# Work that leaves GpSimd, and a planner that models the SBUF port of VectorE and GpSimd

## The chip, the cores and the metric

The kernel runs on one core of one Trainium2 chip. Each engine of the core (TensorE, VectorE, ScalarE, GpSimd, and SyncE for the DMAs) runs its own list of instructions in order; semaphores join them. The metric is the device time of one execution in microseconds (us), as the median of several runs.

## The reference

The program computes two layers of a generative model over 512 latent tokens of width 1024, with 256 context tokens in front, all in float32. Before each layer and each feed-forward network stands an RMSNorm whose scale and shift come from a conditioning vector; after each, a gated residual.

- Layer 0: four heads of bidirectional gated DeltaNet and four heads of bidirectional gated linear attention, in chunks of 64 tokens, over context and latent tokens.
- Layer 1: a Hyena layer. Two long convolutions over 512 positions, `z = gate * long_conv(z, h_fwd, h_bwd, skip)`, whose filters come from a small sine network of the position; the reference takes them by FFT.
- Each layer's feed-forward network: `(silu(u @ w1) * (u @ w3)) @ w2`, with an inner width of 2816.

## The kernel before, in words

**Split products.** A float32 product is made of three faster ones: each operand is split into a rounded part `hi` (ScalarE copies it with a cast) and a rest `lo = x - hi` (VectorE subtracts), and TensorE adds hi·hi, hi·lo and lo·hi in one PSUM bank (`mm3`). So nearly every operand of TensorE costs one ScalarE and one VectorE instruction.

**Order.** Nothing is issued while the program is written down. `Recorder.add` makes an `Op` of each call, with its engine, its dependences and a cost from a formula by engine, operation and size (`cost`, line 404). `schedule` (line 467) then plays the five engines in time: the engine that can start first takes, of the operations that are ready, the one with the best key, which is the longest path of costs behind it plus an offset from the table `BOOST` by section and engine (`"f1@vector"` is VectorE's part of filter chunk 1). DMAs are ordered so too. It also gives out the eight PSUM banks. `issue` writes the instructions out in the order of their planned starts. On the chip that order is fixed for each engine; the true times follow from semaphores. Since `issue` calls every engine from one place, all instructions carry the same line (648) in the profile, and all tiles are named `t` (SBUF) or `bank` (PSUM).

**Stages**, by the time of the profiled execution; neighbours overlap.

- 0 to 250 us: the condition vectors, the input norm, and the Hyena filters in four chunks of 256 channels (`filter_chunk`, sections `f0` to `f3`) for two orders. `fhalf` multiplies four blocks of filter values by a window on VectorE; `mk` (line 937) makes the sum or difference of two blocks, 128x256, on GpSimd: 8 for each chunk and order, 64 in all, 16 of which then overwrite one row with a 1x256 copy. The result is split, `fq` multiplies it by a table of the discrete Fourier transform, and DMAs put the spectra into DRAM (`kscr`). For each chunk and order GpSimd also copies one spectrum (128x256) and one row of it.
- 0 to 600 us: layer 0. `gdn_merge` puts 12 blocks (32x192) a head in place with GpSimd copies, 48 in all, and joins them with small products on TensorE. `gdn_scan` runs both directions of a head chunk by chunk: product, VectorE, product, ScalarE copy `u`, product, VectorE state. For each of its 40 state updates GpSimd scales a block of keys, 128x128, by a column.
- 600 to 1000 and 1300 to 1640 us: the two feed-forward networks. Slices of `w1` and `w3` go through a seven-product scheme of 2x2 blocks (`unit`, line 1830). Of each slice the weight sums S1, S2 and S4 are made on VectorE and the difference S3 (128x512) on GpSimd, 21 for each layer; each is split before TensorE takes it.
- 1000 to 1300 us: Hyena. `project` makes three projections and mirrors blocks of x1 with 16 GpSimd copies, 128x128; `group` transforms, multiplies by the spectra, transforms back and gates. The last gate `y * x2` (128x512) is on GpSimd, 8 times.

Kept on GpSimd in both kernels: the decays, the masks, squares of keys, the gates of layer 0, the sums of products in `conv`, the first gate of Hyena (128x1024) and all memsets.

Of the kernel before, what the change touches and what calls it, by code (L numbers as in the profile page):

```python
# [32 lines left out]
BOOST = {"": 1200, "@gpsimd": 19800, "@vector": -113900, "c": -161700, "c@gpsimd": 173900, "c@sync": -82400,  # L33
         "dft": 21800, "dft@scalar": 56000, "dft@sync": 21800, "dft@vector": -318200, "end": 12900,
         "end@scalar": -111300, "end@sync": -75800, "end@tensor": 253300, "end@vector": 46500, "f0": -3200,
# [19 lines left out]
         "fb@scalar": 22200, "fb@tensor": -4600, "fb@vector": 7200, "ffn0": -123100, "ffn0@scalar": 54200,  # L55
# [5 lines left out]
         "h3@scalar": 117400, "h@sync": 7500, "h@tensor": -117000, "h@vector": -38300, "ht@scalar": 11900,  # L61
         "ht@tensor": 89700, "hy": -14100, "hy@scalar": 26800, "hy@sync": 111000, "hy@tensor": -100100,
         "hy@vector": -3900, "hyout": -1600, "hyout@scalar": -23500, "hyout@sync": -38900, "hyout@vector": -24700,
# [10 lines left out]
         "m15@tensor": 4100, "m15@vector": 55800, "mlp": 9500, "mlp@scalar": 51700, "mlp@sync": -11600,  # L74
         "mlp@tensor": 29000, "modc": 40000, "modc@tensor": -1400, "modc@vector": -2300, "mods": 148900,
         "mods@sync": 12100, "mods@tensor": 6000, "mods@vector": -1900, "n0": 1900, "n0@gpsimd": -6000,
# [3 lines left out]
         "out@scalar": -2900, "out@sync": 7000, "out@tensor": 177300, "p0": -22500, "p0@gpsimd": -483000,  # L80
# [152 lines left out]


class Op:
    __slots__ = ("eng", "calls", "cost", "deps", "succ", "vts", "prio", "path", "idx", "nd", "bytes", "start", "end", "ready", "sec", "tbl", "anc", "alias", "inst", "rows", "first", "last")


class EngineProxy:
# [445 lines left out]
class Kern:  # L685
# [228 lines left out]
    def filter_chunk(s, c):  # L914
# [22 lines left out]
        def mk(h, t, op, fix=None):  # L937
            x = s.t([P, CW])
            (nc.gpsimd.tensor_add if op > 0 else nc.gpsimd.tensor_sub)(x, h[:, t], h[:, 2 + t])
            if fix is not None:  # L940
                nc.gpsimd.tensor_copy(x[:1], fix)
# [1431 lines left out]
```

## Time and profile before

| What | us |
|---|---|
| three runs | 1673.51, 1678.25, 1680.84 |
| their median | 1678.25 |
| profiled execution | 1673.98 |
| its span, first to last instruction | 1672.3 |

The mean granted TensorE clock was 0.972 in it. Its busy times by engine are the first group of rows below.

Busy time is the time in which an engine holds an instruction; one that waits inside an instruction counts as busy. PE is TensorE, DVE VectorE, ACT ScalarE, POOL GpSimd, SP SyncE. The granted clock is a share of 2.4 GHz: 1.0 or 0.5 at any moment, a mean over a stretch. The DMA queue of SyncE moved 199.39 MB, with the 16 DMA engines busy for 39.5% of the span.

### The profile page before, as it was taken

To read this page: it belongs to the slowest core of one execution; us is meant where nothing else is said; L and a number is where in the kernel's file an instruction comes from. 1 tells how busy PE (TensorE), PEld (TensorE's weight loads), DVE (VectorE), ACT (ScalarE), POOL (GpSimd) and SP (SyncE) were. 2 spreads that over 40 slices of the span, in tenths; PEclk is the share of its full clock that TensorE was granted. 3 is DMA by queue.
4 is the path that set the end of the run, shared out by engine and by line. 5 is a ranking of instruction groups with operands and counts; after the bars stand their busy time and mean duration, and the time that the engine had idled before them with its cause. 6 is when DMAs were issued, how large, how long until landed. Compare 5 with 4: busy or idle time off the path is not lost.

```text
span 1672.3 us, 29141 instructions
## 1 busy us (share of the span) xinstructions
PE 1590.1 (95%) x11356; PEld 1400.8 (84%) x11356; DVE 1248.1 (75%) x2158; ACT 791.1 (47%) x1503; POOL 364.9 (22%) x430
## 2 busy tenths in 40 slices
PE   6999889999999889999999999999999999999998
PEld 3687778778777579989989898888889898989898
DVE  4878985657375886968678688598896977868676
ACT  3556533642434444644536365343344653636353
POOL 0344653513232310101010100143440101011000
PEclk9999997998899889999999999999999999999999
DMA  8744332473266432243343354333432333333331
GB/s 284 208 146 152 108 110 68 160 234 112 75 203 211 130 114 64 82 108 90 88 125 95 109 155 134 97 108 92 133 92 76 102 89 101 99 104 98 106 96 56
DMA packets 257147, 201.25 MB, mean 120 GB/s; under 512 B 11281, under 2 KB 234447, under 8 KB 257008
## 3 DMA queue, kind: packets, MB, share of 16 engines
q1 hardware_dynamic: 257008, 199.39, 39.5%
q8 instruction: 89, 1.46, 0.4%
q14 instruction: 50, 0.41, 0.1%
HBM read 185.70 MB, written 13.66 MB: 119 GB/s over the span
## 4 chain that ended last, share of the span: by engine, by line
PE 64%; DVE 21%; ACT 5%; DMA 4%; issue 3%; POOL 3%; SPq 0%; DVEq 0%; POOLq 0%; ACTq 0%
PE bank L648 64%; DVE t L648 21%; ACT t L648 5%; POOL t L648 3%; DMA t<-in_ffn_w_dram 1%; DMA kscr<-t 0%; SPq L648 0%; DMA t<-in_mod_w_dram 0%; ACT L641 0%; DMA t<-in_dft_filt_dram 0%; DMA t<-in_hy_w_in_dram 0%; DMA t<-in_ctx_dram 0%; DMA t<-gscr 0%; DMA t<-in_hy_w_out_dram 0%; DMA t<-in_dft_fwd_dram 0%
## 5 line engine op out<-in xcount | busy, mean ns | idle before, releaser
L648 PE MATMUL bank<-t 128*128 128x256 f32 (+8 forms) x11356 | 1590.1, 316 | 76.2 <-DVE t L648 47.0
L648 PEld LDWEIGHTS bank<-t 128*128 128x128 f32 (+4 forms) x11356 | 1400.8, 183 | 265.3 <-DVE t L648 72.7
L648 DVE TENSOR_TENSOR t<-t 128x512 fp32r<-128x512 f32 (+11 forms) x1151 | 795.7, 728 | 229.3 <-ACT t L648 150.8
L648 ACT CAST t<-t 128x512 fp32r<-128x512 f32 (+4 forms) x651 | 421.6, 664 | 428.7 <-PE bank L648 203.7
L648 POOL TENSOR_TENSOR t<-t 128x256 f32<-128x256 f32 (+3 forms) x230 | 268.5, 1186 | 952.2 <-DMA t<-in_ffn_w_dram 507.8
L648 ACT ACTIVATE t<-t 128x256 f32<-128x256 f32 (+8 forms) x314 | 156.4, 530 | 151.7 <-DVE t L648 132.0
L648 DVE TENSOR_TENSOR t<-bank,t 128x256 f32<-128x256 f32 (+5 forms) x305 | 147.3, 511 | 63.3 <-PE bank L648 50.7
L648 DVE SCALAR_TENSOR_TENSOR t<-bank,t 128x511 f32<-128x511 f32 (+4 forms) x248 | 143.1, 592 | 52.4 <-PE bank L648 35.4
L648 ACT COPY t<-bank 128x256 f32<-128x256 f32 (+2 forms) x272 | 106.8, 408 | 122.7 <-PE bank L648 119.8
L648 ACT ACTIVATE t<-bank 128x256 f32<-128x256 f32 (+7 forms) x134 | 51.0, 389 | 114.3 <-PE bank L648 111.6
L648 ACT ACTIVATE t<-bank,t 128x512 f32<-128x512 f32 (+3 forms) x94 | 51.2, 557 | 57.5 <-PE bank L648 37.4
L648 POOL COPY t<-t 32x192 f32<-32x192 f32 (+3 forms) x96 | 41.7, 440 | 132.9 <-DVE t L648 112.8
L648 DVE SCALAR_TENSOR_TENSOR t<-t 128x256 f32<-128x256 f32 (+7 forms) x134 | 59.4, 494 | 4.3 <-ACT t L648 3.8
L648 DVE SCALAR_TENSOR_TENSOR t<-t,bank 64x128 f32<-64x128 f32 (+1 forms) x112 | 38.0, 345 | 32.1 <-PE bank L648 29.5
L648 DVE COPY t<-bank 128x256 f32<-128x256 f32 (+8 forms) x70 | 31.2, 456 | 24.9 <-PE bank L648 23.4
L648 POOL TENSOR_SCALAR t<-t 128x128 f32<-128x128 f32 x40 | 31.0, 781 | 64.7 <-PE bank L648 31.5
L641 ACT ACT_TABLE_LOAD x32 | 41.1, 1283 | 1.4 <-PEq L2360 0.8
L648 POOL MEMSET t<- 32x192 f32 (+10 forms) x47 | 18.3, 394 | 78.2 <-PE bank L648 58.9
L648 DVE TENSOR_SCALAR t<-t 128x256 f32<-128x256 f32 (+5 forms) x57 | 23.9, 440 | 3.3 <-ACT t L648 2.8
L648 DVE TENSOR_TENSOR_SCAN t<-t 64x768 f32<-64x768 f32 x8 | 14.0, 1750 | 0.2
L648 DVE STREAM_TRANSPOSE t<-t 128x1024 f32<-128x1024 f32 x6 | 10.4, 1755 | 0.3
L648 POOL TENSOR_SCALAR_AFFINE_SELECT t<-t 128x512 f32<-128x512 f32 (+1 forms) x11 | 6.6, 609 | 13.2 <-DVE t L648 13.2
(15 smaller groups left out, 33.6 us busy)
## 6 DMA issues: line engine op xcount, KB each, us to landing
t<-in_mod_w_dram SPq DMA_DIRECT2D x96, 512.0 KB, 4.0
t<-in_ffn_w_dram SPq DMA_DIRECT2D x88, 512.0 KB, 4.1
t<-in_ffn_w_dram SPq DMA_DIRECT2D x48, 384.0 KB, 3.6
t<-in_ab_w_in_dram SPq DMA_DIRECT2D x28, 512.0 KB
t<-in_hy_w_in_dram SPq DMA_DIRECT2D x24, 512.0 KB, 4.3
kscr<-t SPq DMA_DIRECT2D x72, 128.0 KB, 1.8
t<-kscr SPq DMA_DIRECT2D x24, 256.0 KB, 2.6
t<-in_ffn_w_dram SPq DMA_DIRECT2D x16, 256.0 KB, 2.9
```

Source lines behind the costliest of these rows:

```text
L641: s.nc.scalar.add_instruction(mybir.InstLoadActFuncSet(name=s.nc.get_next_instruction_name(), engine=mybir.EngineType.Activation, act_func ...
L648: r = getattr(getattr(s.nc, o.eng), name)(*[b(x) for x in a], **{n: b(x) for n, x in k.items()})
```

## The change

Five things change.

1. `cost` gives an operation a mark `lock`: on VectorE, where it has more than one SBUF input (columns of scalars not counted), or copies or scales one SBUF tensor without PSUM; on GpSimd, for all but memsets. `schedule` then starts a marked operation no earlier than the planned end of the last marked one on the other engine.
2. The 64 sums of `mk` go from GpSimd to VectorE.
3. The 42 differences S3 and the 8 gates `y * x2` go from GpSimd to VectorE.
4. All copies of `mk`, of the spectrum, of `gdn_merge` and of the mirrored x1 go from GpSimd to ScalarE, and so do the 40 scaled keys of `gdn_scan` (as an activation with a column of scales).
5. The table `BOOST` holds other offsets, for nearly all sections. So the order changes on all engines and in the DMA queue, also far from the moved operations.

```diff
-BOOST = {"": 1200, "@gpsimd": 19800, "@vector": -113900, "c": -161700, "c@gpsimd": 173900, "c@sync": -82400,
...
+BOOST = {"": 65700, "@vector": -50900, "c": -5300, "c@gpsimd": -159000, "c@sync": -2500, "dft": 4600,
...
         elif eng == "vector":
+            sb = sum(1 for x in ins if not isinstance(x, View) and (len(x.shape) > 2 or x.shape[1] > 1))
+            op.lock = op.lock or sb > 1 or (sb == 1 and not ps and name in ("tensor_copy", "tensor_scalar"))
...
         else:
+            op.lock = name not in ("memset",)
...
+        port = {"vector": 0.0, "gpsimd": 0.0}
...
+            if o.lock:
+                t = max(t, port["gpsimd" if e == "vector" else "vector"])
+                port[e] = t + c
             o.start, o.end = t, t + c
...
         def mk(h, t, op, fix=None):
-            (nc.gpsimd.tensor_add if op > 0 else nc.gpsimd.tensor_sub)(x, h[:, t], h[:, 2 + t])
+            (nc.vector.tensor_add if op > 0 else nc.vector.tensor_sub)(x, h[:, t], h[:, 2 + t])
             if fix is not None:
-                nc.gpsimd.tensor_copy(x[:1], fix)
+                nc.scalar.copy(x[:1], fix)
...
-            nc.gpsimd.tensor_copy(kd, kc0)
-            nc.gpsimd.tensor_copy(kd[:1], kny[:1])
+            nc.scalar.copy(kd, kc0)
+            nc.scalar.copy(kd[:1], kny[:1])
...
-            nc.gpsimd.tensor_copy(X[sl, 0, :, sl], Xt[sl, 0:6])
-            nc.gpsimd.tensor_copy(X[sl, 1, :, sl], Xr[sl, 6:12])
+            nc.scalar.copy(X[sl, 0, :, sl], Xt[sl, 0:6])
+            nc.scalar.copy(X[sl, 1, :, sl], Xr[sl, 6:12])
...
-            nc.gpsimd.tensor_copy(aux[sl, :, c], Xr[sl, 0:6] if b < 2 else Xt[sl, 6:12])
+            nc.scalar.copy(aux[sl, :, c], Xr[sl, 0:6] if b < 2 else Xt[sl, 6:12])
...
-                    nc.gpsimd.tensor_scalar(kd, ktok[:, t], s.kdf[:, d, t, h:h + 1], None, ALU.mult)
+                    nc.scalar.activation(kd, ktok[:, t], AF.Copy, scale=s.kdf[:, d, t, h:h + 1])
...
-                add("S3", nc.gpsimd, "tensor_sub", A11, A21)
+                add("S3", nc.vector, "tensor_sub", A11, A21)
...
-                nc.gpsimd.tensor_copy(xr[:, 0], xT[:, 255:127:-1])
-                nc.gpsimd.tensor_copy(xr[:, 1], xT[:, 511:383:-1])
+                nc.scalar.copy(xr[:, 0], xT[:, 255:127:-1])
+                nc.scalar.copy(xr[:, 1], xT[:, 511:383:-1])
...
-                nc.gpsimd.tensor_mul(y, y, x2[:, c])
+                nc.vector.tensor_mul(y, y, x2[:, c])
```

## Rows read from the trace of the kernel before

**Rows 1.** The page's head and section 1 (busy us, share of the span, instructions).

```profile
span 1672.3 us, 29141 instructions
...
PE 1590.1 (95%) x11356; PEld 1400.8 (84%) x11356; DVE 1248.1 (75%) x2158; ACT 791.1 (47%) x1503; POOL 364.9 (22%) x430
```

**Rows 2.** Windows: length, busy per engine (instructions), granted clock, DMA share, GB/s.

```profile
0.00:250.00 250.00, 212.74 (x1387) 168.26 (x1388) 196.77 (x435) 128.53 (x275) 99.98 (x132) 0.98 0.53 168
250.00:600.00 350.00, 332.43 (x2753) 265.56 (x2752) 222.61 (x435) 151.65 (x267) 115.70 (x163) 0.90 0.46 147
600.00:720.00 120.00, 111.35 (x838) 105.27 (x838) 100.57 (x172) 67.58 (x135) 13.59 (x7) 0.99 0.30 85
720.00:1000.00 280.00, 279.36 (x1950) 261.15 (x1949) 207.05 (x299) 134.62 (x260) 24.41 (x16) 1.00 0.38 109
1000.00:1300.00 300.00, 292.18 (x1825) 258.72 (x1824) 240.77 (x386) 126.36 (x210) 79.67 (x92) 1.00 0.36 107
1300.00:1340.00 40.00, 36.17 (x278) 35.47 (x278) 36.21 (x59) 25.18 (x51) 6.20 (x4) 0.92 0.35 97
```

**Rows 3.** Chain of waits by line, of 0:250, 250:600, 600:720, 1000:1300.

```profile
by line: DVE t L648 43.7%; PE bank L648 11.9%; POOL t L648 9.0%; ACT t L648 7.8%; issue 6.6%; DMA kscr<-t 3.2%; SPq L648 3.2%; DMA t<-in_mod_w_dram 3.0%; DMA t<-in_dft_filt_dram 2.8%; DMA t<-in_ctx_dram 2.1%; DMA t<-gscr 1.9%; ACT L641 1.9%
...
by line: PE bank L648 64.7%; DVE t L648 24.2%; ACT t L648 5.3%; issue 3.9%; POOL t L648 1.2%; ACT L641 0.7%; DVEq L648 0.0%; ACTq L648 0.0%
...
by line: DVE t L648 36.2%; PE bank L648 36.2%; ACT t L648 13.7%; DMA t<-in_ffn_w_dram 6.7%; issue 4.5%; POOL t L648 2.8%; DVEq L648 0.1%; POOLq L648 0.0%; SPq L648 0.0%
...
by line: PE bank L648 57.2%; DVE t L648 26.0%; issue 4.5%; POOL t L648 3.9%; ACT t L648 3.7%; DMA t<-in_ffn_w_dram 2.9%; DMA t<-in_hy_w_in_dram 1.7%; DMA t<-in_hy_w_out_dram 1.5%; DVEq L648 0.1%; POOLq L648 0.0%; ACTq L648 0.0%
```

**Rows 4.** Groups by line and shape, POOL and DVE in 0:250 (mean in ns).

```profile
L648 POOL TENSOR_TENSOR t<-t 128x256 f32<-128x256 f32 x64 | 55.6, 889 | 107.4 <-DVE t L648 104.0 <-ACT t L648 3.2
L648 POOL COPY t<-t 1x256 f32<-1x256 f32 x24 | 15.5, 644 | 2.0 <-ACT t L648 1.5
...
L648 POOL COPY t<-t 128x256 f32<-128x256 f32 x8 | 5.2, 654 | 15.8 <-ACT t L648 15.8
...
L648 DVE TENSOR_TENSOR t<-t 128x256 fp32r<-128x256 f32 x81 | 40.8, 526 | 9.4 <-ACT t L648 9.0
...
L648 DVE TENSOR_TENSOR t<-t 1x256 f32<-1x256 f32 x16 | 11.0, 688 | 0.0
```

**Rows 5.** The same view, whole run.

```profile
L648 DVE TENSOR_TENSOR t<-t 128x256 f32<-128x256 f32 x100 | 42.2, 439 | 14.6 <-ACT t L648 6.7 <-DMA t<-in_hy_filt_out_dram 4.9 <-DMA kscr<-t 1.7
...
L648 POOL TENSOR_SCALAR t<-t 128x128 f32<-128x128 f32 x40 | 31.0, 781 | 64.7 <-PE bank L648 31.5 <-ACT t L648 20.8 <-DVE t L648 7.9
...
L648 POOL COPY t<-t 32x192 f32<-32x192 f32 x48 | 16.8, 350 | 3.9 <-DVE t L648 1.7
...
L648 ACT ACTIVATE t<-bank,t 128x128 f32<-128x128 f32 x24 | 8.8, 367 | 22.0 <-PE bank L648 21.9
...
L648 ACT ACTIVATE t<-bank 32x192 f32<-32x192 f32 x24 | 6.8, 316 | 9.8 <-PE bank L648 9.6
```

**Rows 6.** The same view, POOL in 620:1000.

```profile
L648 POOL TENSOR_TENSOR t<-t 128x512 f32<-128x512 f32 x21 | 34.2, 1632 | 315.2 <-DMA t<-in_ffn_w_dram 269.9 <-DVE t L648 45.3
```

**Rows 7.** The same view, POOL in 1000:1300.

```profile
L648 POOL TENSOR_TENSOR t<-t 128x512 f32<-128x512 f32 x8 | 11.2, 1415 | 14.4 <-DVE t L648 14.2
```

**Rows 8.** Timeline 733:741: start, us, engine, operation, count [idle before].

```profile
739.40 0.69 DVE L648 TENSOR_TENSOR t<-t 128x512 f32<-128x512 f32 x1 [2.52 <-ACT t L648]
```

**Rows 9.** Timeline 752.5:757.

```profile
752.81 4.11 DVE L648 TENSOR_TENSOR t<-t 128x512 f32<-128x512 f32 x3 [2.82 <-DMA t<-in_ffn_w_dram]
752.94 3.42 POOL L648 TENSOR_TENSOR t<-t 128x512 f32<-128x512 f32 x2 [41.56 <-DMA t<-in_ffn_w_dram]
```

**Rows 10.** Timeline 704:719.

```profile
708.01 3.37 POOL L648 TENSOR_TENSOR t<-t 128x512 f32<-128x512 f32 x1 [9.82 <-DMA t<-in_ffn_w_dram]
```

**Rows 11.** Timeline 232:246.

```profile
238.55 4.79 POOL L648 TENSOR_SCALAR t<-t 128x128 f32<-128x128 f32 x3
...
245.09 1.27 PE L648 MATMUL bank<-t 128*128 128x128 f32 x6 [3.30 <-ACT t L648]
```

More of the change, by code (lines that the diff above doesn't have):

```diff
@@ L32 @@
 CW = 256
-BOOST = {"": 1200, "@gpsimd": 19800, "@vector": -113900, "c": -161700, "c@gpsimd": 173900, "c@sync": -82400,
-         "dft": 21800, "dft@scalar": 56000, "dft@sync": 21800, "dft@vector": -318200, "end": 12900,
-         "end@scalar": -111300, "end@sync": -75800, "end@tensor": 253300, "end@vector": 46500, "f0": -3200,
[19 rows of a table removed]
-         "fb@scalar": 22200, "fb@tensor": -4600, "fb@vector": 7200, "ffn0": -123100, "ffn0@scalar": 54200,
[5 rows of a table removed]
-         "h3@scalar": 117400, "h@sync": 7500, "h@tensor": -117000, "h@vector": -38300, "ht@scalar": 11900,
-         "ht@tensor": 89700, "hy": -14100, "hy@scalar": 26800, "hy@sync": 111000, "hy@tensor": -100100,
-         "hy@vector": -3900, "hyout": -1600, "hyout@scalar": -23500, "hyout@sync": -38900, "hyout@vector": -24700,
[10 rows of a table removed]
-         "m15@tensor": 4100, "m15@vector": 55800, "mlp": 9500, "mlp@scalar": 51700, "mlp@sync": -11600,
-         "mlp@tensor": 29000, "modc": 40000, "modc@tensor": -1400, "modc@vector": -2300, "mods": 148900,
-         "mods@sync": 12100, "mods@tensor": 6000, "mods@vector": -1900, "n0": 1900, "n0@gpsimd": -6000,
[3 rows of a table removed]
-         "out@scalar": -2900, "out@sync": 7000, "out@tensor": 177300, "p0": -22500, "p0@gpsimd": -483000,
[15 rows of a table removed]
-         "vec": -17400, "vec@scalar": -72600, "vec@sync": -1400, "vec@tensor": 1000, "vec@vector": 10000,
[7 rows of a table removed]
@@ new lines @@
+BOOST = {"": 65700, "@vector": -50900, "c": -5300, "c@gpsimd": -159000, "c@sync": -2500, "dft": 4600,
+         "dft@scalar": -55500, "dft@sync": -1500, "dft@vector": -316700, "f0": 14400, "f0@gpsimd": -1300,
[18 rows of a table added]
+         "fb3o@tensor": -65500, "fb@scalar": 500, "fb@sync": -70500, "fb@tensor": -9000, "fb@vector": -300,
[6 rows of a table added]
+         "h@tensor": 1000, "h@vector": 142400, "ht@scalar": 11900, "ht@tensor": 89700, "hy@scalar": -104400,
+         "hy@sync": 168400, "hy@tensor": -86600, "hy@vector": -82900, "hyout": -800, "hyout@scalar": 93300,
+         "hyout@sync": -1000, "hyout@tensor": -79400, "hyout@vector": -8400, "i0@gpsimd": 500, "i0@scalar": -46000,
+         "i0@vector": -1000, "i2": 600, "i2@gpsimd": 300, "i2@scalar": 46200, "i2@vector": -86400, "in": -192800,
+         "in@scalar": 106100, "in@sync": -20800, "in@tensor": -180000, "in@vector": -105500, "l0": -3500,
[8 rows of a table added]
+         "m15@vector": 55800, "mlp": 112500, "mlp@scalar": 35700, "mlp@sync": -9600, "mlp@tensor": -116600,
+         "mlp@vector": 80500, "modc": -21500, "modc@sync": -11400, "modc@tensor": -9500, "modc@vector": 162800,
+         "mods": 44500, "mods@sync": -900, "mods@tensor": 4900, "mods@vector": -16900, "n0@gpsimd": -30300,
[27 rows of a table added]
@@ L235 @@
 class Op:
-    __slots__ = ("eng", "calls", "cost", "deps", "succ", "vts", "prio", "path", "idx", "nd", "bytes", "start", "end", "ready", "sec", "tbl", "anc", "alias", "inst", "rows", "first", "last")
+    __slots__ = ("eng", "calls", "cost", "deps", "succ", "vts", "prio", "path", "idx", "nd", "bytes", "start", "end", "ready", "sec", "tbl", "anc", "alias", "inst", "rows", "first", "last", "lock")
 class EngineProxy:
@@ L351, in add @@
             op.eng, op.calls, op.cost, op.deps, op.succ, op.vts, op.prio, op.idx = eng, [], 0.0, set(), [], {}, s.boost + BOOST.get(f"{s.sec}@{eng}", 0.0), len(s.ops)
-            op.bytes, op.tbl, op.sec, op.alias, op.inst, op.rows, op.first, op.last = 0, None, s.sec, set(), None, P, None, None
+            op.bytes, op.tbl, op.sec, op.alias, op.inst, op.rows, op.first, op.last, op.lock = 0, None, s.sec, set(), None, P, None, None, False
             s.ops.append(op)
@@ L629, in warm @@
         o.eng, o.calls, o.vts, o.alias, o.tbl, o.idx = "tensor", [("matmul", (View(v)[:, :P],), dict(lhsT=x, rhs=x, start=True, stop=True))], {v: True}, (), None, -1
-        o.cost, o.start, o.inst, o.sec, o.bytes, o.deps = P * 4 / 2.4, start, None, "warm", 0, ()
+        o.cost, o.start, o.inst, o.sec, o.bytes, o.deps, o.lock = P * 4 / 2.4, start, None, "warm", 0, (), False
         return o
```

118 rows, old and new, of the table BOOST are left out of this document.

## The prediction, made before the changed kernel ran

> **What bounds the kernel now.** I read the page's head first: TensorE is busy for 1590.1 of 1672.3 us, VectorE for 1248.1, GpSimd for 364.9 [rows 1]. Such a mean hides stages, so the windows come next [rows 2]. In the feed-forward stretch 720 to 1000 TensorE is busy for 279.36 of 280 us at full clock: nothing that helps another engine there can shorten it, and the second network looks alike. From 0 to 250 it is idle for 37.3 us, from 250 to 600 for 17.6 us, and there the granted clock is 0.90, which means that a fifth of the stretch ran at the lower of its two levels. From 600 to 720 it is idle for 8.7 us, from 1000 to 1300 for 7.8, from 1300 to 1340 for 3.8. So what can be won lies before 720 and in the short heads of the stages.
>
> The chain of waits tells on whom TensorE waits [rows 3]. From 0 to 250, VectorE has 43.7% of it (109 us) and GpSimd 9.0% (22.5 us); TensorE itself 11.9%. From 250 to 600 it is 24.2% (85 us) and 1.2% (4.2 us); from 600 to 720, 36.2% (43 us) and 2.8% (3.4 us); from 1000 to 1300, 26.0% (78 us) and 3.9% (11.7 us). GpSimd has 42 us in all, VectorE some 315 in these four.
>
> **What GpSimd does to VectorE.** A difference of 128x512 takes VectorE 0.69 us where GpSimd is still [rows 8]. With two of GpSimd's beside them, three such take 4.11 us, not 2.1, and the two take 3.42 us [rows 9]: one engine stands while the other runs. In 0 to 250 the same shows in the means: 81 rests of 128x256 took 526 ns each [rows 4] where sums of that size average 439 over the whole run [rows 5], so at least 81 x 0.087 = 7.0 us of standing; 16 operations on one single row took 688 ns, longer than 128 rows, so at least 16 x 0.25 = 4.0 us more [rows 4]. Together 11 us of VectorE's busy time there is waiting.
>
> The Trainium skill (SBUF — State Buffer, "Who interferes with whom") says that a VectorE instruction with two SBUF inputs and a GpSimd instruction that reads SBUF exclude each other: one "fully blocks". The pair of 4.11 and 3.42 us agrees [rows 9]. By that rule moved work costs the shared port only VectorE's shorter time; I return to it as a rival.
>
> **The change, part by part.**
>
> *Filter sums to VectorE (0 to 250).* GpSimd loses 55.6 us of sums, 15.5 and 5.2 us of copies in this stage [rows 4]. Of its 22.5 us on the chain I leave 2.5 to what stays (the decays) and take 20 off; this holds a jam at 238.55, where three scaled keys hold GpSimd for 4.79 us ahead of the last sum and TensorE then stands for 3.30 us [rows 11]. VectorE gains 64 x 0.439 = 28.1 us [rows 4, 5]. It is on the chain for 109 of its 196.77 busy us, 55%, so I charge 15.5 us; at worst all 28.1, at best nothing, in its 53 idle us. The 11 us of standing go too, at 55% 6. The 24 one-row copies and 8 spectrum copies go to ScalarE; no row shows its one-row copy, and between nothing and 367 ns, the time of its 128x128 scaling [rows 5], I take 0.37 us: 12 us, of which the chain's 7.8% x 250 / 128.53 = 15% gives 2. Sum: -20 + 15.5 - 6 + 2 = -8.5 us. Late next behind the sum are ScalarE's cast and VectorE's rest, as before.
>
> *Merge copies and scaled keys to ScalarE (250 to 600).* GpSimd loses 16.8 and 31.0 us. ScalarE gains 48 x 0.316 = 15.2 and 40 x 0.367 = 14.7 us, priced by its nearest rows, which read PSUM [rows 5]. It is busy for 151.65 of 350 us and has 5.3% of the chain (18.6 us, 12% of its busy time): of 29.9 us I charge 3.7; all on the path would be 29.9. Queued behind a scaled key on ScalarE is the copy `u` on which the next state product waits; but the key depends on no state and can be made early, and 198 us of ScalarE's time is idle. Of 4.2 us of GpSimd on the chain I take 3 off. Sum: about +1 us; by the bounds from -4 to +30.
>
> *S3 to VectorE (the networks).* 21 of 1.632 us leave GpSimd in the first network [rows 6], as many in the second, and VectorE gains 42 x 0.69 = 29.0 us [rows 8]. Where TensorE is full, this moves nothing: VectorE is busy for 207.05 of 280 us there [rows 2], and loses more standing than it gets work. If that cover were gone, 29 us would be the price. At the head of the first network it is different: one S3 at 708.01 takes 3.37 us, through five VectorE differences [rows 10], and GpSimd has 3.4 us of that stretch's chain [rows 3]. At 0.69 us this returns 2.7 us; as much at the head of the second network, where VectorE is busy for 36.21 of 40 us [rows 2]. For both heads -5, with the few S3 that VectorE then makes itself already taken off the 3.37.
>
> *Last gates and mirrored copies (1000 to 1300).* 8 gates leave GpSimd at 1.415 us [rows 7] for 0.69 on VectorE. Most are not needed until the output projection; only the last pair ends a chain: -2 us, bounds 0 and 8 x 0.73 = -6. VectorE's 5.5 us more lie in its 59 idle us. The 16 copies cost ScalarE under 16 x 0.367 = 6 us of its 174 idle ones: 0. The 128x1024 gates stay, so most of GpSimd's 11.7 us on the chain stays.
>
> *The mark and the offsets.* The mark costs the chip nothing: it alters an order. Before, the planner let both engines run at once in places such as 752.81, so VectorE's real times ran behind its plan. With the mark those orders fit better, and the new offsets shuffle all queues, SyncE's too. No row shows an order that isn't there yet. I bound it by the 72 us for which TensorE stood up to 1300 (37.3 + 17.6 + 8.7 + 7.8) plus 35 us at half clock (0.10 x 350, in the reckoning of full-speed time), 107 us, to the better, and the same count on the other side cannot be excluded, though a loss of all the 20 us won above is the likelier floor. I take a tenth, -11.
>
> Sum: -8.5 + 1 - 5 - 2 - 11 = -25.5 us. From the profiled execution's 1673.98 us that is 1648.5. The median of the runs shown lies 4.3 us higher, so a median may come out nearer 1653; I say 1649.
>
> **Rivals.**
>
> *The port was the larger part.* If the port excludes, as the pair shows, all that leaves GpSimd frees the difference of durations. From 0 to 250 that is 55.6 - 28.1 plus 15.5 + 5.2 = 48 us [rows 4]; if VectorE's half of the chain is stretched by it all, 55% or 26 us go where I took 8.5, and a plan that fits the chip gives a fifth of 107, 21 us. With -5, -2 and +1: -53, 1621 us. For it: the jams at 752.81 and 708.01. Against: GpSimd has only 22.5 us of that chain. This is where the skill's rule would lead.
>
> *The next wait takes over.* The freed GpSimd time returns as VectorE time: -20 turns into -5 because all 28.1 us of sums lie on the path, and the order gives nothing: -20 + 28.1 - 6 + 2 + 1 - 5 - 2 = -2, so 1672 to 1677 us. For it: VectorE's 43.7% of the chain is twice any other's. Against: the sums on VectorE need no hop between engines.
>
> *Slower: VectorE becomes the bound of the filter stage.* Its queue runs in order. If the 28.1 us come on top, the standing doesn't go because what stays on GpSimd still meets VectorE, and half of the 64 sums wait behind one more 0.439 us operation (14 us), the stage gets 28.1 + 14 - 20 + 2 = 24 us longer; the rest gives -6: 1692 us. It decides once VectorE is busy for more than some 90% of the stage; it is at 79% and 28.1 us make 90%. Against: the standing ought to fall.
>
> **How the numbers follow.** Under 0.5%, 8 us, this kernel's runs can't tell from no change (they spread over 7 us): faster is below 1670, slower above 1687. Forecast (1630 to 1668) 0.55; port the larger part (below 1632) 0.13, both faster; next wait (1670 to 1687) 0.18; slower 0.14. Range: 1620 to 1688, which leaves 0.06 below and 0.13 above; the forecast's own range is 1630 to 1668.
>
> **What would show it.** GpSimd's busy time near 160 us (364.9 - 55.6 - 15.5 - 5.2 - 31.0 - 16.8 - 34.2 twice, nearly, - 11.2 - 4 of mirrored copies). VectorE's differences near 0.69 us in the networks, rests of 128x256 near 430 ns before 250. GpSimd under 4% of the chain from 0 to 250, TensorE's idle time there below 30 us, networks as long as before. I am wrong if the stretch to 720 isn't shorter though GpSimd leaves the chain, if VectorE passes 90% before 250, or if the gain lies in the networks.

## The result, and the profile after

The changed kernel took 1635.92 us as the median of four runs, against 1676.57 us before: a ratio of 0.976, 95% interval 0.9726 to 0.9793. That is 41 us faster; forecast were 1649 us, with a range of 1620 to 1688. The profiled execution has a span of 1634.4 us, 38 us shorter than that of before [rows 1].

The page's head and section 1 of after:

```profile
span 1634.4 us, 29362 instructions
...
PE 1586.8 (97%) x11538; PEld 1411.3 (86%) x11538; DVE 1229.3 (75%) x2272; ACT 832.3 (51%) x1637; POOL 155.9 (10%) x180
```

GpSimd's busy time fell from 364.9 to 155.9 us, near the 160 of the prediction. VectorE has 62 us of new work (64 x 0.428 + 50 x 0.686, rows below) and is yet busy for 19 us less, so the work that it kept takes some 81 us less; the rows below show standing gone from it. TensorE has 182 more products: dummy ones that the planner puts into gaps (`warm`). They count as busy, so not all of the idle time that goes is gain. The mean granted clock is 0.972 as before.

The same stretches as in [rows 2] (length, busy time of TensorE, weight loads, VectorE, ScalarE and GpSimd with instructions, granted clock, DMA share, GB/s). A stretch holds a little more of the work now, as the kernel is ahead:

```profile
0.00:250.00 250.00, 229.09 (x1661) 183.56 (x1661) 201.62 (x522) 139.74 (x319) 16.26 (x28) 0.95 0.69 217
250.00:600.00 350.00, 334.27 (x2689) 272.93 (x2690) 235.19 (x445) 187.94 (x356) 78.80 (x84) 0.91 0.39 121
600.00:720.00 120.00, 118.87 (x936) 115.42 (x935) 92.64 (x166) 67.90 (x139) 0.00 (x0) 1.00 0.28 76
720.00:1000.00 280.00, 278.90 (x1978) 261.99 (x1976) 209.81 (x348) 140.61 (x276) 0.00 (x0) 1.00 0.41 118
1000.00:1300.00 300.00, 298.25 (x1932) 269.53 (x1932) 249.93 (x399) 137.26 (x240) 60.85 (x68) 1.00 0.35 104
```

TensorE's idle time from 0 to 250 fell from 37.3 to 20.9 us, from 600 to 720 from 8.7 to 1.1, from 1000 to 1300 from 7.8 to 1.8. VectorE is at 81% of the first stretch, not at the 90% from which the slower rival decides.

The chain of waits by line of after, of 0:250, 250:600, 600:720 and 1000:1300, against [rows 3]:

```profile
by line: PE bank L654 41.9%; DVE t L654 32.4%; ACT t L654 5.6%; SPq L654 4.4%; DMA t<-in_window_dram 3.8%; issue 3.7%; DMA t<-in_hy_filt_out_dram 3.2%; DMA kscr<-t 2.2%; DMA t<-in_mod_w_dram 2.0%; ACT L647 0.5%; DVEq L654 0.0%; ACTq L654 0.
...
by line: PE bank L654 62.4%; DVE t L654 25.7%; ACT t L654 6.8%; issue 4.2%; ACT L647 0.8%; POOL t L654 0.4%; DVEq L654 0.0%; ACTq L654 0.0%
...
by line: PE bank L654 74.5%; DVE t L654 12.5%; ACT t L654 12.5%; issue 0.7%; DVEq L654 0.0%
...
by line: PE bank L654 75.4%; DVE t L654 15.6%; ACT t L654 4.2%; DMA t<-in_ffn_w_dram 3.1%; issue 1.9%; DVEq L654 0.0%; ACTq L654 0.0%
```

GpSimd is off the chain but for 0.4% of 250:600. There little changed; in the other three VectorE's share went from 43.7% to 32.4%, 36.2% to 12.5% and 26.0% to 15.6%, and TensorE's own rose from 11.9% to 41.9%, 36.2% to 74.5% and 57.2% to 75.4%.

VectorE's groups in 0:250 of after (mean ns of one behind the comma), to be read against [rows 4]: sums of 128x256, the 64 among them, take 428 ns on VectorE, the rests of 128x256 fell from 526 to 412, the operations on one row from 688 to 477.

```profile
L654 DVE TENSOR_TENSOR t<-t 128x256 f32<-128x256 f32 x82 | 33.3, 428 | 4.4 <-DMA t<-in_hy_filt_out_dram 1.8 <-PE bank L654 1.4 <-DMA kscr<-t 1.0
L654 DVE TENSOR_TENSOR t<-t 128x256 fp32r<-128x256 f32 x81 | 32.2, 412 | 3.1 <-ACT t L654 2.6
...
L654 DVE TENSOR_TENSOR t<-t 1x256 f32<-1x256 f32 x16 | 7.6, 477 | 0.9 <-DMA kscr<-t 0.8
```

And its differences of 128x512 in 720:1000, S3 among them:

```profile
L654 DVE TENSOR_TENSOR t<-t 128x512 f32<-128x512 f32 x80 | 53.0, 686 | 18.4 <-DMA t<-in_ffn_w_dram 10.1 <-ACT t L654 8.2
```

ScalarE's moved work over the whole run of after. From SBUF a block of 32x192 takes 349 ns and a scaled key 397, where the prediction priced them at 316 and 367 by rows that read PSUM [rows 5]; a copy of a single row takes as long as a whole scaled key:

```profile
L654 ACT COPY t<-t 32x192 f32<-32x192 f32 x48 | 16.8, 349 | 5.8 <-DVE t L654 5.2
...
L654 ACT ACTIVATE t<-t 128x128 f32<-128x128 f32 x40 | 15.5, 397 | 9.7 <-PE bank L654 5.0 <-DMA kscr<-t 2.6 <-DVE t L654 1.5
...
L654 ACT COPY t<-t 1x256 f32<-1x256 f32 x24 | 9.6, 400 | 2.5 <-DVE t L654 2.3
```

**Where the time came from.** Two long runs of TensorE, one in each feed-forward network, are marks that all kernels share. The chain of waits shows them as its longest pieces (start, length, engine, instructions). Before:

```profile
719.56 267.54 PE bank L648 x1848
...
1334.04 303.56 PE bank L648 x2123
```

After:

```profile
692.85 267.55 PE bank L654 x1848
...
1298.17 300.90 PE bank L654 x2123
```

The first run begins 26.7 us earlier. From its end to the start of the second lie 346.9 us before (719.56 + 267.54 to 1334.04) and 337.8 after: Hyena and the heads on both sides gave 9.1 us. The second run is 2.7 us shorter; the first is not.

### The profile page after: what moved, and what is told of

Its sections match the earlier page's. It is cut to its first block, busy times and chain, and to the rows that moved or that the text cites. A ratio compares the mean times of both kernels' runs of the same rounds, so it can differ in the third digit from the quotient of the medians.

```text
span 1634.4 us, 29362 instructions
## 1 busy us (share of the span) xinstructions
PE 1586.8 (97%) x11538; PEld 1411.3 (86%) x11538; DVE 1229.3 (75%) x2272; ACT 832.3 (51%) x1637; POOL 155.9 (10%) x180
## 4 chain that ended last, share of the span: by engine, by line
PE 75%; DVE 15%; ACT 5%; DMA 3%; issue 2%; SPq 1%; POOL 0%; DVEq 0%; ACTq 0%
PE bank L654 75%; DVE t L654 15%; ACT t L654 4%; SPq L654 1%; DMA t<-in_window_dram 1%; DMA t<-in_ffn_w_dram 1%; DMA t<-in_hy_filt_out_dram 0%; DMA kscr<-t 0%; DMA t<-in_mod_w_dram 0%; DMA t<-in_dft_fwd_dram 0%; ACT L647 0%; POOL t L654 0%; DVEq L2374 0%; DVEq L654 0%; ACTq L654 0%
## 5 line engine op out<-in xcount | busy, mean ns | idle before, releaser
L654 PE MATMUL bank<-t 128*128 128x256 f32 (+6 forms) x11538 | 1586.8, 313 | 41.0 <-DVE t L654 20.7
L654 DVE TENSOR_TENSOR t<-t 128x512 fp32r<-128x512 f32 (+12 forms) x1265 | 788.8, 664 | 220.6 <-ACT t L654 129.4
L654 ACT CAST t<-t 128x512 fp32r<-128x512 f32 (+3 forms) x651 | 420.2, 665 | 414.1 <-PE bank L654 214.9
L654 ACT ACTIVATE t<-t 128x256 f32<-128x256 f32 (+7 forms) x354 | 170.4, 515 | 126.9 <-DVE t L654 107.6
L654 POOL TENSOR_TENSOR t<-t 128x256 f32<-128x256 f32 (+3 forms) x116 | 130.5, 1149 | 721.7 <-DVE t L654 624.5
L654 DVE TENSOR_TENSOR t<-bank,t 128x512 f32<-128x512 f32 (+5 forms) x305 | 147.6, 513 | 67.9 <-PE bank L654 43.4
L654 DVE SCALAR_TENSOR_TENSOR t<-t 128x256 f32<-128x256 f32 (+6 forms) x134 | 55.7, 469 | 3.8 <-ACT t L654 3.4
L654 DVE COPY t<-bank 128x256 f32<-128x256 f32 (+6 forms) x70 | 31.3, 459 | 30.2 <-PE bank L654 29.2
L654 ACT COPY t<-t 32x192 f32<-32x192 f32 (+3 forms) x96 | 33.7, 358 | 14.2 <-DVE t L654 13.2
```

What stands on the lines that cost most here:

```text
L654: r = getattr(getattr(s.nc, o.eng), name)(*[b(x) for x in a], **{n: b(x) for n, x in k.items()})
```

## The experiments

The new placement and the new order came together. They can be parted, since the planner's order can be kept while an operation is issued on another engine: the call gets the engine on which it is issued, and costs and order are made from the one on which it is planned. TensorE's and the DMA queue's instructions are then the same, one by one.

```diff
     def add(s, eng, name, a, k):
...
+        op.emit = k.pop("_on", None)
         op.calls.append((name, a, k))
...
     def issue(s, order, banks):
...
-                r = getattr(getattr(s.nc, o.eng), name)(...)
+                e = o.eng
+                if o.emit is not None:
+                    e, name, k = o.emit
+                r = getattr(getattr(s.nc, e), name)(...)
```

Theory A: the durations and the standing at the port are what counts. Theory B: the order is. All times are medians; ratios are to before, run beside it, with 95% intervals. "First run" is the start of TensorE's first long run, "between" the time from its end to the second's start, both read from the chain as above, of one execution each. The start is the looser of the two: executions of one order can differ by 7 us there (shown at h_early), while the time between is 337.8 to 338.3 us in the four kernels of after's order that leave S3 and the last gates on VectorE.

| Kernel | order planned for | moved work runs on | us | ratio | first run | between |
|---|---|---|---|---|---|---|
| before | before | GpSimd | 1676.57 | 1 | 719.6 | 346.9 |
| c_filt | before | filters moved | 1667.98 | 0.9961 (0.9945 to 0.9976) | 712.4 | 349.2 |
| c_act | before | ScalarE's part moved | 1683.85 | 1.0056 (1.0038 to 1.0074) | 722.6 | 350.0 |
| c_all | before | all moved | 1672.72 | 0.9983 (0.9967 to 0.9999) | 719.0 | 347.0 |
| p_newO | after, no mark | all moved | 1653.91 | 0.988 (0.9862 to 0.9898) | 697.3 | 346.9 |
| p_l_oldO | mark, old offsets | all moved | 1669.74 | 0.9979 (0.996 to 0.9997) | 721.3 | 340.7 |
| h_early | mark, late offsets old | all moved | 1639.14 | 0.9784 (0.976 to 0.9808) | 700.1 | 339.9 |
| g_l_newO | mark, new offsets | GpSimd | 1665.14 | 0.9936 (0.9905 to 0.9968) | 719.2 | |
| d_all | after | GpSimd | 1650.63 | 0.9864 (0.984 to 0.9888) | 702.7 | 341.1 |
| d_filt | after | filters back | 1648.53 | 0.9848 (0.9821 to 0.9876) | 706.2 | 337.8 |
| d_S3 | after | S3 back | 1643.96 | 0.9821 (0.9802 to 0.984) | 701.1 | 340.1 |
| d_act | after | ScalarE's part back | 1634.73 | 0.975 (0.9726 to 0.9773) | 689.0 | 338.3 |
| d_merge | after | merge copies back | 1628.11 | 0.9718 (0.9692 to 0.9743) | 683.1 | 337.8 |
| after | after | all moved | 1635.92 | 0.976 (0.9726 to 0.9793) | 692.9 | 337.8 |

### The placement alone, in the old order (c_all)

```diff
-            (nc.gpsimd.tensor_add if op > 0 else nc.gpsimd.tensor_sub)(x, h[:, t], h[:, 2 + t])
+            (nc.gpsimd.tensor_add if op > 0 else nc.gpsimd.tensor_sub)(x, h[:, t], h[:, 2 + t], _on=("vector", "tensor_add" if op > 0 else "tensor_sub", {}))
...
-                nc.gpsimd.tensor_copy(x[:1], fix)
+                nc.gpsimd.tensor_copy(x[:1], fix, _on=("scalar", "copy", {}))
```

and the other moved calls in the same way.

> The order of before, instruction for instruction on TensorE and in the DMA queue; only the 178 moved sums, differences, gates, copies and scaled keys are issued on VectorE and ScalarE, at the place in time that the plan had for them on GpSimd. Theory A (the durations and the standing at the port are what counts): most of the 41 us come without any new order, 1645 to 1655 us, with VectorE's 128x512 operations at 0.69 us in the networks and GpSimd off the chain before 250 us. Theory B (the new order is what counts, the moved work little): 1662 to 1672 us, the -14.5 us of the prediction's steps without the order or less. Rival C (VectorE's queue is overloaded before 250 us once the sums are there): 1680 us or more.

Measured: 3 us faster, 0.9983 (it is 250 operations that move, the 430 of GpSimd less the 180 left to it, and not 178). Theory A falls as it was put; theory B holds, 0.7 us outside its range. In c_all's chain the first run begins where it did, and the second run has the length of after's:

```profile
719.04 267.45 PE bank L653 x1847
...
1333.48 300.65 PE bank L653 x2123
```

### The order alone (d_all)

The converse edit in after: the calls are planned on VectorE and ScalarE and issued on GpSimd.

> The converse: the order of after, but the moved work is issued on GpSimd again, at the places that the plan had for it on VectorE and ScalarE. Theory A: 1660 to 1670 us, some 25 us slower than after, with GpSimd near 360 us busy and VectorE's standing back. Theory B: 1640 to 1650 us, since the order alone carries the gain.

1650.63 us, just above the range of theory B: with GpSimd nearly as busy as before (356.1 us), the order alone is worth 25 us. The placement is worth the 15 us from there to after, five times what it is worth in the old order.

### The old offsets in the new planner (p_l_oldO), and the old placement in it (g_l_newO)

p_l_oldO is after with the table `BOOST` of before; g_l_newO is after with all the calls of the diff back on GpSimd, and planned there.

```diff
-BOOST = {"": 65700, "@vector": -50900, "c": -5300, "c@gpsimd": -159000, "c@sync": -2500, "dft": 4600,
+BOOST = {"": 1200, "@gpsimd": 19800, "@vector": -113900, "c": -161700, "c@gpsimd": 173900, "c@sync": -82400,
...
-                add("S3", nc.vector, "tensor_sub", A11, A21)
+                add("S3", nc.gpsimd, "tensor_sub", A11, A21)
...
```

The first pair of lines is of p_l_oldO, the second of g_l_newO.

> After with the old table of offsets: the work is moved and the planner knows the port, and it plans anew with the old offsets. Theory A: 1638 to 1652 us, the offsets being of little weight. Theory B: 1660 us or more, as the offsets belong to one plan and lose their sense in another; it may even be slower than before.

> After's planner and offsets, but all the work stays on GpSimd, and is planned there. Theory A: 1655 to 1680 us, since the port's standing and GpSimd's long sums are still there. Theory B: 1640 to 1655 us if the offsets carry over; if offsets fit only the plan that they were made for, 1670 us or more, and then this run alone doesn't tell A from B.

1669.74 us, theory B, and 1665.14 us, in the range of theory A but not near what theory B asks of offsets that carry over. The first run begins at 721.3 and 719.2 us in them, where it did before. So neither the new offsets nor the new placement by itself gives the 26.7 us up to there, or any large part of them: they need offsets and placement that were planned together. The time between the runs is shorter in both all the same; the next run says why.

### Without the mark (p_newO)

```diff
-            if o.lock:
+            if False:
                 t = max(t, port["gpsimd" if e == "vector" else "vector"])
```

> After without the planner's mark: the work is moved and the new offsets stand, but the plan lets VectorE and GpSimd run together. Theory A (the mark makes the plan true, and that is worth the 11 us or more): 1650 us or more. Theory B (little is left on GpSimd, so the mark matters little; the offsets carry it): 1633 to 1645 us. Theory C (offsets fit one plan only, and any change of the planner's rules spoils them): 1660 to 1675 us, like p_l_oldO.

Theory A holds: 18 us slower than after by the medians. The profiled execution, the fastest of its five, is 12.6 us longer by the spans: 4.4 before the first run, no more than executions of one order differ by, and the time between the runs is back at 346.9 us:

```profile
697.25 267.54 PE bank L654 x1848
...
1311.67 300.66 PE bank L654 x2123
```

All five kernels whose order was planned without the mark have 346.9 to 350.0 us between the runs, those with it 337.8 to 341.1, with either offsets and wherever the work runs (g_l_newO's second run begins with other products, so it can't be read so). They are two orders without the mark, before's and this one, and three with it. As p_newO takes out nothing else, Hyena's 9 us hang on the mark. Which instructions it puts in a better place there isn't shown.

### The placement by parts, in the old order (c_filt, c_act)

c_filt moves the filter sums and the filter copies alone, c_act the merge copies, scaled keys and mirrored copies.

> The order of before, with the 64 filter sums on VectorE and the 32 copies of the filter stage on ScalarE alone; merge copies, scaled keys, S3 and last gates stay on GpSimd. In c_all, TensorE was 7 us ahead of before at 250 us and level again at 500 us. Theory A (ScalarE's new copies and keys between 250 and 500 us ate it): here the 7 us stay, 1666 to 1670 us. Theory B (in the fixed order another chain holds layer 0, and being early in the filters is worth nothing): level again at 500 us, 1673 to 1677 us.

> The order of before, with only the 48 merge copies, 40 scaled keys and 16 mirrored copies moved to ScalarE. Theory A: 4 to 7 us slower than before, 1680 us or more, lost between 250 and 500 us. Theory B: within 3 us of before, 1673 to 1679 us; the prediction's step charged 1 us for it.

Theory A of both holds, c_act's by more than its 4 to 7 us: the filters give 7 us, ScalarE's new work takes 9. The two can't be added up, since both remove the jam of [rows 11]. TensorE's list is the same in before, c_filt and c_act, so the starts of its products can be compared one by one. At the product that before starts at 236 us, c_filt is 3.0 us ahead and c_act 1.6; at that of 252 us they are 9.2 and 7.3 us ahead. In between before's TensorE stands for 3.30 us, and from 244.6 to 251.4 us its granted clock is at the lower level. In c_filt (first line) and c_act (second), timeline 232:252, there is no such wait:

```profile
238.68 10.36 PE L653 MATMUL bank<-t 128*128 128x128 f32 x76 [0.26 <-ACT t L653]
...
238.31 12.69 PE L653 MATMUL bank<-t 128*128 128x256 f32 x93 [1.21 <-DVE t L653]
```

In c_filt the lower level comes later, from 250.8 us on; at the product of 270 us it is 6.6 us ahead, and stays near that. So about half of the filters' 7 us is this one jam, and c_act, which leaves the sums on GpSimd, is rid of it too. VectorE makes the 64 sums in c_filt for 2.8 us more of busy time from 0 to 250 us (196.77 in [rows 2]):

```profile
0.00:250.00 250.00, 217.25 (x1434) 172.62 (x1434) 199.60 (x515) 141.20 (x312) 28.18 (x39) 0.99 0.55 173
```

S3 and the last gates were not moved alone in this order. In the chain of 250:530 ScalarE has 6.1% of 280 us before

```profile
by line: PE bank L648 70.0%; DVE t L648 17.5%; ACT t L648 6.1%; issue 3.9%; POOL t L648 1.5%; ACT L641 0.9%; ACTq L648 0.0%; DVEq L648 0.0%
```

and twice that in c_act, 18 us more:

```profile
by line: PE bank L653 58.1%; DVE t L653 17.0%; ACT t L653 12.7%; issue 5.8%; DMA kscr<-t 2.3%; DMA t<-in_mod_w_dram 2.1%; POOL t L653 1.5%; ACT L643 1.4%; DMA t<-gscr 1.3%; ACTq L653 0.0%; POOLq L653 0.0%; DVEq L653 0.0%; SPq L653 0.0%
```

The timeline of c_act shows the place, the joining of the first two heads' blocks: seven copies in a row hold ScalarE for 2.41 us, behind them stand another activation and three more copies, and only then come the sign changes (`ACTIVATE` of 32x192 from a bank) on whose blocks TensorE's next products work. TensorE stands for 2.18 us until just behind the first of them (the profile names no releaser there) and, after more copies, for 0.40 us, which it puts down to ScalarE.

```profile
258.10 2.41 ACT L653 COPY t<-t 32x192 f32<-32x192 f32 x7
...
262.46 0.54 ACT L653 ACTIVATE t<-bank 32x192 f32<-32x192 f32 x2
...
262.88 2.79 PE L653 MATMUL bank<-t 64*64 64x64 f32 x24 [2.18 <-issue]
...
266.07 1.28 PE L653 MATMUL bank<-t 64*64 64x64 f32 x10 [0.40 <-ACT t L653]
```

### Single parts back on GpSimd, in the new order (d_S3, d_filt, d_act, d_merge)

```diff
-            nc.scalar.copy(X[sl, 0, :, sl], Xt[sl, 0:6])
+            nc.scalar.copy(X[sl, 0, :, sl], Xt[sl, 0:6], _on=("gpsimd", "tensor_copy", {}))
```

is one of the three lines of d_merge; the others are made alike.

> The order of after, with only the 42 differences S3 issued on GpSimd. Where TensorE is full they should cost nothing, and some us at the heads of the two networks: the prediction's step says 5 us, so 1639 to 1643 us; if the whole network stretch suffers, as the long last run of TensorE in before suggests (303.6 us against 300.9), 3 us more. If the heads no longer depend on S3 in the new order: as after, 1636 us.

> The order of after, with the 64 filter sums and the 32 copies of the filter stage on GpSimd again. In the order of before this move was worth 7 us; the prediction's step says 8.5 us. Theory A (worth the same in any order): 1642 to 1646 us, the lead lost before 250 us and not won back. Theory B (in the new order the filters are filler and not on the path): 1634 to 1639 us.

> The order of after, with the 48 merge copies, 40 scaled keys and 16 mirrored copies on GpSimd; filter sums, S3 and last gates stay on VectorE. In the order of before this move to ScalarE cost 9 us. Theory A (ScalarE's queue pays for it in any order): faster than after by 5 to 9 us, 1627 to 1631 us, a version better than both. Theory B (the new order was planned with these on ScalarE, so there they are hidden, and on GpSimd they come later than planned): 1637 to 1645 us.

> The order of after, with only the 48 merge copies on GpSimd. Theory A: some 3 to 6 us faster than after, since the trace of c_act shows TensorE waiting behind these copies on ScalarE. Theory B: within 3 us of after, 1633 to 1639 us.

S3 back costs 8 us by the medians; the first long run takes 267.54 us again. How much of the 8 us is S3's own is not clear. In the profiled execution of d_S3 TensorE's products are already 5.8 us behind those of after when the first S3 starts,

```profile
644.05 1.72 POOL L659 TENSOR_TENSOR t<-t 128x512 f32<-128x512 f32 x1 [49.65 <-PE bank L659]
```

and up to there the two kernels' lists are the same on every engine. From 385 to 430 us its granted clock was 0.65, after's 0.73. Behind the first S3 come 2.4 us up to the first long run and 2.1 to the end of the second. The filters back cost 13 us, more than in the old order and beyond the range of theory A. ScalarE's part back changes nothing within the intervals, which is neither of its theories; but its merge copies alone back give 8 us, theory A by more than its 6: d_merge is the fastest kernel of the study. Its interval and after's overlap by a little (0.9726 to 0.9743); four of its five runs lie under all of after's, the spans are 1624.3 and 1634.4 us, and the first run begins 9.8 us earlier:

```profile
683.08 267.54 PE bank L659 x1848
...
1288.37 300.66 PE bank L659 x2123
```

Two stretches hold the joining of blocks, one for two heads each (columns as above). After:

```profile
240.00:320.00 80.00, 77.32 (x673) 64.34 (x672) 43.51 (x91) 50.54 (x114) 18.83 (x23) 0.81 0.25 81
...
385.00:430.00 45.00, 41.74 (x506) 32.29 (x505) 17.44 (x36) 19.96 (x54) 2.26 (x7) 0.73 0.52 164
```

d_merge:

```profile
240.00:320.00 80.00, 74.60 (x710) 62.63 (x711) 50.52 (x105) 44.34 (x93) 31.68 (x50) 0.94 0.32 105
...
385.00:430.00 45.00, 44.00 (x542) 34.30 (x535) 18.20 (x35) 16.31 (x41) 14.34 (x35) 0.85 0.59 189
```

The granted clock, between the levels of 1.2 and 2.4 GHz, is 0.81 and 0.73 with the copies on ScalarE and 0.94 and 0.85 with them on GpSimd. On ScalarE all 24 of the first two heads stand ahead of the sign changes, which begin 11.7 us behind the first small products (`MATMUL` of 32x32); pieces of after's timeline:

```profile
250.56 24.74 PE L654 MATMUL bank<-t 32*32 32x32 f32 x275 [1.19 <-DVE t L654]
...
254.59 4.31 ACT L654 COPY t<-t 32x192 f32<-32x192 f32 x12
...
259.77 2.51 ACT L654 COPY t<-t 32x192 f32<-32x192 f32 x7
...
262.30 0.88 ACT L654 ACTIVATE t<-bank 32x192 f32<-32x192 f32 x3
```

and of d_merge's, where 24 copies run beside ScalarE and the sign changes begin 6.6 us behind those products:

```profile
253.21 4.30 PE L659 MATMUL bank<-t 32*32 32x32 f32 x57 [1.24 <-DVE t L659]
253.22 4.91 POOL L659 COPY t<-t 32x192 f32<-32x192 f32 x10 [24.10 <-DVE t L659]
...
259.83 0.88 ACT L659 ACTIVATE t<-bank 32x192 f32<-32x192 f32 x3
...
261.29 3.76 POOL L659 COPY t<-t 32x192 f32<-32x192 f32 x7
```

Compared product by product with after, d_merge gains 7.4 us between the products of 249 and 285 us and 5.1 between those of 398 and 410; a second execution of after's order (h_early, below) gains 1.1 and nothing there. So the gain lies at the joining.

d_act's median lies 6.6 us above d_merge's, so the scaled keys and mirrored copies seem better on ScalarE; no run has them alone. d_act gains 6.9 and 2.7 us in the same two places, and 3.8 us are lost again between the products of 422 and 428 us, where h_early, with the keys on ScalarE, loses 3.9 as well. What the keys are worth stays open.

### The old offsets for the late stages (h_early)

```diff
-BOOST = {"": 65700, ..., "fa0": 23900, "fa0@gpsimd": -28000, ..., "p0": -2900, "p0h": -8100, ...}
+BOOST = {"": 65700, ..., "fa0": 162900, "fa0@gpsimd": 49100, ..., "p0": -2900, "p0h": -13300, ...}
```

> After with the new offsets up to the loading of the residual stream (filters, layer 0, modulation vectors), and the old offsets from the output projection of layer 0 on (networks and Hyena). If the order's gain adds up by stage, the early part keeps what after won before its first long run of TensorE (27 us) and the late part loses some 9 us: 1642 to 1650 us, with that run beginning at 690 to 696 us as in after. If offsets only work as one set: 1660 us or more, with the run beginning at 710 us or later.

1639.14 us, 3 us from after, which the intervals can't tell from nothing, and below the range expected for stages that add up. The profile has the first run begin 7.2 us later than in after:

```profile
597.46 44.45 PE bank L585 x312
...
700.06 267.55 PE bank L585 x1848
```

where after has, beside its first run at 692.85 us,

```profile
591.91 42.90 PE bank L654 x312
```

But up to 694 us h_early's lists are after's, shape by shape, on all engines and in the DMA queue. So these 7 us are not the offsets' work: they are what two executions of one order differ by, and this one was the slowest of its five (1644.84 us). Its granted clock in the two stretches at the joining of blocks was 0.87 and 0.67, where after had 0.81 and 0.73:

```profile
240.00:320.00 80.00, 72.79 (x673) 61.28 (x676) 44.53 (x97) 48.98 (x111) 18.16 (x21) 0.87 0.28 92
385.00:430.00 45.00, 42.15 (x487) 32.43 (x486) 17.85 (x38) 19.66 (x53) 2.26 (x7) 0.67 0.47 148
```

Between the runs it has 339.9 us. The new offsets of networks and Hyena are worth 3 us at most by the medians; with all old offsets (p_l_oldO) the kernel is 34 us slower than after, so those of filters and layer 0 carry the order's gain.

## Why the prediction was right, and where its steps were off

**The sign, the range and most signs in the profile** were right: GpSimd at 156 us, off the chain, VectorE's 128x512 differences at 0.69 us, TensorE's idle time before 250 us under 30, the first network's long run as long as before. The measured 1635.92 us lie 13 us below the forecast of 1649.

**Filter sums, -8.5 us.** c_filt measured -7, d_filt -13 in the new order. That GpSimd's hop and jam leave the chain stood as put, but the sum came near by luck. It charged VectorE 15.5 us for the sums and gave 6 back; c_filt shows 2.8 us more of busy time. It took 20 us off for GpSimd; about half of the 7 measured in the old order is the one jam of [rows 11].

**ScalarE's part, +1 us.** In the old order it cost 9, though it removed the jam; in the new one nothing can be told from 0 for the whole, but the merge copies alone cost 8. The bounds of -4 to +30 held. What failed in the step is the place: it looked for harm at the copy `u` behind the scaled keys. The harm lay at the sign changes behind the merge copies, which GpSimd had made beside ScalarE.

**S3, -5 us, and the gates, -2 us.** d_S3 measured 8 us, with the first network's full stretch untouched as predicted; in the profiled execution 4.5 us of its delay lie behind the start of the first S3, close to the 5. The gates were not measured alone. The five differences through which [rows 10] was read are, in the same timeline,

```profile
707.15 3.08 DVE L648 TENSOR_TENSOR t<-t 128x512 f32<-128x512 f32 x5
```

The first network's long run is 267.5 us with S3 on either engine; the second's was 303.6 us in before, 300.7 in c_all and in d_S3.

**The order, -11 us.** This is the term that was mis-sized. It measured 25 us with the work on GpSimd (d_all) and 37 with it moved (from c_all to after). It was a tenth of 107 us by choice; no row of before set that share. Two things in it can be told apart now: the mark, worth 18 us by the medians, 9 of them between the networks and the rest not placed, and offsets made for this placement, without which nothing that shows is won before the first network.

**The sum.** The four steps of placement came to -14.5 us; in the new order they measured 15 us, in the old one 3. They aren't worth a fixed time. That an early result waits for its old place in the queue, where the order was made for GpSimd's times, is the likely reason; no run shows it for single operations. The rival in which the port was the larger part (1621 us) had the same two causes; it put 26 us on the filters, where 7 to 13 were measured, and 21 us on the order. The time of c_all, 1672.72 us, is that of the rival in which the next wait takes over, though by another way: VectorE did not pay for the sums, ScalarE's queue did for its copies.

What stays open: why the new offsets fit. They were changed in nearly all sections at once, and only two sets of sections were parted. Open too: where the mark's other 9 us lie.

## What to carry to other kernels

Where a program's order is planned from costs, a moved operation is worth little until the order is planned anew; run the new placement in the old order, and the old in the new, before naming either as the cause. A planner that knows which engines exclude each other can be worth its trouble where both have work, here 9 us in one stage. Before a difference of a few us in one stage is read from a profile, see what two executions of one order differ by there, here up to 7 us where the granted clock falls. Small copies on an engine that also empties PSUM for the next product belong on an idle engine even if each takes as long there.

## What the runs showed of the hardware

VectorE's rests of 128x256 before 250 us took 412 ns once GpSimd had 28 instructions left in the stage, 526 with its 132; the port cost VectorE more than the 7 us that the prediction read from the means (81 x 0.114 = 9.2 us). The Trainium skill (SBUF — State Buffer, "Who interferes with whom") says that ScalarE never waits for another engine's port. This agrees with the scaled keys at 397 ns and the merge copies at 349 ns in after, and 399 and 349 in c_act. So its operations did not get longer, and what ScalarE's new work cost lies in its queue.
